# Hybrid encoder step on one core: seven operations of the attention stage change engine or place

## The chip, the cores and the metric

The kernel runs on one core of a Trainium2 chip. The metric is the device time of one execution in microseconds (us), first to last instruction with what lies around it. Engines are named as in the profile: PE is TensorE (PEld its weight loads), DVE is VectorE, ACT is ScalarE, POOL is GpSimd, SP is SyncE, which issues the DMAs here.

## What is computed

One layer is applied to 2048 prompt rows and to 8 sample sequences of 16 rows with 512 cached keys each. This is the reference, cut to the part that the change touches.

```python
def _layer(x, past_k, past_v, ...):
    p = _rms_norm(x, g_pre_mix) @ w_in          # [u | v | q | k | v], 512 columns each
    u_a = gelu(p[..., :512])
    v_a = _layer_norm(gelu(p[..., 512:1024]), ln_v_g, ln_v_b)
    out_a = u_a * (tril(W_s) @ v_a + b)          # gating, chunks of 128 rows, 4 heads
    out_b = _stick_breaking(q, [past_k, k], [past_v, v])   # 8 heads x 64
    mix = concat(_rms_norm(out_a), _rms_norm(out_b)) @ w_out
    x = x + _rms_norm(mix)
    ...                                          # then a convolutional FFN
def _stick_breaking_block(q, k, v):
    z = q @ k.T * 64 ** -0.5
    log_fail = where(reach, log_sigmoid(-z), 0)
    excl = reversed cumulative sum of log_fail, exclusive
    return where(reach, exp(log_sigmoid(z) + excl), 0) @ v
```

## The kernel before

The kernel has four stages, which the profile shows one after the other: the input projection (to about 400 us), attention with the gating branch mixed into it (about 400 to 1126 us), the output projection (to about 1430 us) and the FFN (the rest). Every product of weights and activations that has to be exact in fp32 is made of three fp32r products of a high and a low half (`mm3`, L267 to L269): the high half is a rounding copy, made on ACT, and the low half is the source minus the high half.

**Prompt attention.** `prompt_unit` treats one head, one section of keys and one block of 128 query rows. Its four parts run at a lag to each other in the loop at L863: `pre` six units ahead, `weights_`, `transposes` three units later, `values` after that. `weights_` calls `weigh` (L529): PE makes scores z (L680), ACT makes S = sigmoid(-z) (L543) and s = sigmoid(z) (L544), DVE makes the reversed running product of S in place (L546, a scan) and multiplies s by S shifted by one column (L548). POOL puts the one column at the end of S: a memset to 1 (L536), or a copy of the column `left` (L538) that an earlier section of the same rows left (L688, DVE). `transposes` turns s by PE (L697) and ACT copies it out to T (L698). `values` (L700) multiplies by V for two heads, gg = 0 and 1, each into its own 64 rows of the PSUM tile po (L712 to L715); DVE copies po to ob (L722), which is stored.

**Sample attention.** Eight `sample_unit`s lie among the units of the first head pair. `pre` clears the block-diagonal queries qb on POOL (L565) and fills them from qs by four copies of 64 x 64 (L568), loads cached keys into kr in two parts, rounds them on ACT (L582), takes the low half (L583), and adds the new keys by two small copies (L587). kr has one buffer, so the second part is loaded when the first has been read. `values` copies pos out on ACT (L630), turns it by PE (L632) and writes the two halves into obs (L635).

**Gating.** `gating` is a generator whose steps are spread between the prompt units. `fetch` loads one 128-row block of x into xr (one buffer), rounds it on ACT (L815), takes the low half xl (L816), and 24 products per block follow (L829 to L831); `fetch` of the next block is written ahead of the products of this one. `gate_chain` finishes each block; its one POOL step is rs (L781), on which a DVE step (L783) depends.

The order on each engine is settled at build time by a scheduler that works on a timing model of its own. Within an engine instructions run in that order, and one that waits holds up those behind it. `keep_in_program_order`, used at L582 and L583, keeps an instruction at its written place.

Of the kernel before, what the change touches and what calls it, by code (L numbers as in the profile page):

```python
# [14 lines left out]
F32 = mybir.dt.float32  # L15
F32R = mybir.dt.float32r
AF = mybir.ActivationFunctionType
ALU = mybir.AluOpType
# [8 lines left out]
NB, NS = 8, 16  # L27
# [26 lines left out]
def hybrid_kernel(ctx: ExitStack, tc: tile.TileContext, a: dict):  # L54
    nc = tc.nc
# [4 lines left out]
    def load(out, in_):  # L60

        with ExitStack() as c:
            if loaded:
                c.enter_context(tc.issue_after(loaded[-1]))
            loaded.append(dma(out, in_).ins)
# [24 lines left out]
    ks = lpool.tile([P, 2, 4, NSAMP], F32R, name="ks")  # L90
# [427 lines left out]
    with ExitStack() as c2:  # L518
# [35 lines left out]
        obs = fil.tile([P, 4, NSAMP], F32, name="obs")  # L554

        def sample_unit(b):

            W = PAST + NS
            H = W // 2
            st = {}  # L560

            def pre():
                qb = [fil.tile([P, KD * P], F32R, tag=t, name="qb", bufs=2)[:, :640] for t in ("xh", "xl")]
                for hl in range(2):
                    nc.gpsimd.memset(qb[hl].bitcast(F32), 0.0)  # L565
                    for g in range(2):
                        rows = slice(g * 64, g * 64 + 64)
                        nc.vector.tensor_copy(  # L568
                            qb[hl][rows].rearrange("p (k c) -> p k c", c=160)[:, :, g * NS:(g + 1) * NS],
                            qs[rows, hl, :, b * NS:(b + 1) * NS].bitcast(F32))  # L570
                vnew = fil.tile([P, 512], F32, tag="va", name="vnew", bufs=2)[:NS]
                load(vnew, v_s.parts(b * NS, (b + 1) * NS)[0][0])
                vc = fil.tile([P, 4, 512], F32, tag="ub", name="vc", bufs=2)
                k = []
                for c in range(2):
                    k0, k1 = c * H, min((c + 1) * H, PAST)
                    n = k1 - k0
                    kr = fil.tile([P, 4 * H], F32, tag="xr", name="kr").rearrange("p (k n) -> p k n", k=4)[:, :, :n]
                    load(kr, a["ckT"][b][:, :, k0:k1])
                    hi, lo = (fil.tile([P, 4 * H], F32R, tag=f"fw{2 * c + i}", name=f"ck{i}").rearrange(  # L580
                        "p (k n) -> p k n", k=4) for i in range(2))
                    tc.keep_in_program_order(nc.scalar.copy(hi[:, :, :n], kr))  # L582
                    tc.keep_in_program_order(nc.vector.tensor_tensor(  # L583
                        out=lo[:, :, :n], in0=kr, in1=hi[:, :, :n].bitcast(F32), op=ALU.subtract))
                    if n < H:
                        for hl, kk in enumerate((hi, lo)):
                            nc.vector.tensor_copy(kk[:, :, n:], ks[:, hl, :, b * NS:(b + 1) * NS].bitcast(F32))  # L587
                    k.append((hi, lo))
                load(vc, a["cv"][b])
                st["k"], st["v"] = (qb, k), (vc, vnew)  # L590

            def weights_():
                qb, k = st["k"]

                def fill(z, c0, cn):
                    hi, lo = k[c0 // H]
                    for kt in range(4):
                        q0, q1 = (q[:, kt * P:(kt + 1) * P] for q in qb)
                        mm3(z, q0, q1, hi[:, kt], lo[:, kt], kt == 0, kt == 3 and not c0)
                    if c0:  # L600
                        nc.tensor.matmul(z[:, PAST - c0:], lhsT=identr, rhs=hidesmp, start=False, stop=True)

                st["w"] = weigh(W, H, fill, None)[0]

            def transposes():
                w = st["w"]
                wT = st["wT"] = fil.tile([P, 8 * P], F32, tag="nhl", name="wTs").rearrange("p (j c) -> p j c", c=P)
                pt = pst.tile([P, 4, P], F32, tag="pt", name="pt")
                for j in range(4):
                    nc.tensor.transpose(pt[:, j], w[:, j * P:(j + 1) * P], ident)  # L610
                nc.scalar.copy(wT[:, :4], pt)
                pt = pst.tile([P, 4, P], F32, tag="pt", name="pt")
                nc.tensor.transpose(pt[:NS, 0], w[:, PAST:W], ident)
                nc.scalar.copy(wT[:NS, 4], pt[:NS, 0])

            def values(part):

                if part:
                    return
                vc, vnew = st["v"]  # L620
                wT = st["wT"]
                po = pso.tile([P, 256], F32, tag="po", name="pos")[:, :P]
                for j in range(5):
                    kn = P if j < 4 else NS
                    for kt in range(4):
                        cs = slice(kt * P, (kt + 1) * P)
                        nc.tensor.matmul(po[kt * 32:(kt + 1) * 32], lhsT=wT[:kn, j, kt * 32:(kt + 1) * 32],
                                         rhs=vc[:, j, cs] if j < 4 else vnew[:, cs], start=(j == 0), stop=(j == 4))
                o = fil.tile([P, 512], F32, tag="o", name="os", bufs=2)[:, :P]
                nc.scalar.copy(o, po)  # L630
                pt = pst.tile([P, 4, P], F32, tag="pt", name="pt")
                nc.tensor.transpose(pt[:, 0], o, ident)  # L632
                for g in range(2):
                    rows = slice(g * 64, g * 64 + 64)
                    nc.vector.tensor_copy(obs[rows, :, b * NS:(b + 1) * NS], pt[rows, 0].rearrange(  # L635
                        "p (k c) -> p k c", c=32)[:, :, g * NS:(g + 1) * NS])
                if b == NB - 1:
                    dma(ob_s.parts(0, NSAMP)[0][0].rearrange("f p n -> p f n"), obs)

            return pre, weights_, transposes, values  # L640

        def sections(pr):
# [7 lines left out]
        def prompt_unit(hp, pr, sec, i, g, shared):  # L650
# [3 lines left out]
            n = min(b1, t + 1) - b0  # L654
# [45 lines left out]
            def values(part):  # L700

                if g == 0 or i == 0:
                    return
                cut = [b0 + n * p // NPART for p in range(NPART + 1)]
                if part == 0 and own:
                    shared["po", pr] = pso.tile([P, 2 * P], F32, tag="po", name="po")
                po = shared["po", pr]
                for j in range(cut[part], cut[part + 1]):
                    q = slice(P if j == t else 0, 2 * P)
                    last = j == (b1 - 1 if b0 == 0 else -1)  # L710
                    first_ = own and j == b0
                    for gg in range(2):  # L712
                        T = shared["T", pr, b0 + (j - b0) // 4 * 4, gg]
                        nc.tensor.matmul(po[gg * 64:gg * 64 + 64, q], lhsT=shared["V"][:, j, gg * 64:(gg + 1) * 64],  # L714
                                         rhs=T[:, (j - b0) % 4, q], start=first_, stop=last)  # L715
                if part < NPART - 1 or b0:
                    return
                if ("ob", c) not in shared:
                    shared["ob", c] = two.tile([P, 512], F32, tag="ob", name="ob")
                    shared["n", c] = 0  # L720
                ob = shared["ob", c]
                nc.vector.tensor_copy(ob[:, (pr % 2) * 256:(pr % 2 + 1) * 256], po)  # L722
                shared["n", c] += 1
                if shared["n", c] == 2:
                    dma(ob_s.parts(cs.start, cs.stop)[0][0][hp], ob)

            return pre, weights_, transposes, values, W


# [65 lines left out]
        def gating():  # L795
# [14 lines left out]
            def fetch(i):  # L810
                xr = fil.tile([P, 1056], F32, tag="xr", name="xr")[:, :KD * P].rearrange("p (k n) -> p k n", n=P)
                load(xr, a["xT"][:, :, i * P:(i + 1) * P])
                hi, lo = (fil.tile([P, KD * P], F32R, tag=t, name=t, bufs=2).rearrange("p (k n) -> p k n", n=P)
                          for t in ("xh", "xl"))
                nc.scalar.copy(hi, xr)  # L815
                nc.vector.tensor_tensor(out=lo, in0=xr, in1=hi.bitcast(F32), op=ALU.subtract)  # L816
                return hi, lo

            x = fetch(0)
            n = 0  # L820
            for i in range(NTT):
                if n == 0:
                    n = m = 4 if i < 8 else 3
# [3 lines left out]
                for k in range(KD):  # L827
                    hi, lo, w = x[0][:, k], x[1][:, k], uw[k]
# [501 lines left out]
```

## Time and profile before

| | us |
|---|---|
| median of 3 runs | 2996.64 (2992.61 to 2998.26) |
| the profiled execution: its own time | 2994.9 |
| the profiled execution: span from first to last instruction | 2993.1 |
| PE busy in the span | 2869.0 (96%) |
| DVE busy | 1892.8 (63%) |
| ACT busy | 1347.1 (45%) |
| POOL busy | 343.6 (11%) |

The shares are means over four stages that differ: the FFN is half of the span and keeps PE's weight loads busy nearly all of the time, and the attention stage does not. A PE that is busy by the profile is not a PE at its peak, since matmuls are pipelined and their ends are modelled; the busy share of PEld tells more.

### The profile page before, as it was taken

How to read it: one execution, taken by the hardware profiler on the slowest of the kernel's cores; microseconds unless marked ns; L12 is line 12 of the kernel's file. 1: busy time of each engine (PE TensorE's matmuls, PEld its weight loads, DVE VectorE, ACT ScalarE, POOL GpSimd, SP SyncE). 2: the span in 40 equal slices, each digit the busy share in tenths (PEclk: the TensorE clock that was granted, in tenths of full speed). 3: DMA queues.
4: the chain of work that ended last, by engine and by line, in shares of the span. 5: the costliest groups of instructions: out<-in, count | busy, mean ns of one | idle time of the engine just before them, and what ended most of it. 6: DMA issues, size and time to landing. Idle time of an engine off the chain costs nothing.

```text
span 2993.1 us, 44223 instructions
## 1 busy us (share of the span) xinstructions
PE 2869.0 (96%) x17070; PEld 2627.3 (88%) x17070; DVE 1892.8 (63%) x2840; ACT 1347.1 (45%) x2391; POOL 343.6 (11%) x487
## 2 busy tenths in 40 slices
PE   8999988889999998999999999999999999999997
PEld 7999876657666667999999999899999999999997
DVE  7666668887988894876444555763444476344445
ACT  5444447777767774543332233433232243323222
POOL 0000011011111111552000000310000030000002
PEclk9999989999999999999999999999999999999998
DMA  7767854422434326655222212542212133211223
GB/s 244 241 231 240 255 170 123 117 82 71 126 94 119 86 64 203 225 197 187 67 69 73 64 61 73 152 124 76 70 50 71 61 114 116 78 57 60 75 64 109
DMA packets 242673, 356.06 MB, mean 119 GB/s; under 512 B 26528, under 2 KB 172192, under 8 KB 241440
## 3 DMA queue, kind: packets, MB, share of 16 engines
q1 hardware_dynamic: 242464, 353.24, 38.1%
q8 instruction: 135, 2.21, 0.3%
q14 instruction: 74, 0.61, 0.1%
HBM read 285.66 MB, written 67.51 MB: 118 GB/s over the span
## 4 chain that ended last, share of the span: by engine, by line
PE 79%; DVE 8%; DMA 4%; ACT 4%; issue 3%; POOL 1%; SPq 1%; DVEq 0%; ACTq 0%; POOLq 0%
PE pu L268 12%; PE pu L267 12%; PE pu L269 12%; PE pd L267 5%; PE pd L268 5%; PE pd L269 5%; PE po L714 3%; DVE S L546 3%; PE pt L697 2%; PE psf L267 2%; PE psf L268 2%; PE psf L269 2%; PE z L680 2%; PE pst L385 2%; PE pst L386 2%
## 5 line engine op out<-in xcount | busy, mean ns | idle before, releaser
L185 DVE TENSOR_TENSOR wlo<-wr,whi 128x1024 fp32r<-128x1024 f32 (+2 forms) x325 | 354.3, 1090 | 569.3 <-ACT whi L184 566.9
L267 PE MATMUL pu<-hhi,whi 128*128 128x364 f32 (+1 forms) x2112 | 696.0, 330 | 3.6 <-ACT nhs L1114 3.6
L268 PE MATMUL pu<-hlo,whi 128*128 128x364 f32 (+1 forms) x2112 | 696.8, 330 | 0.0
L269 PE MATMUL pu<-hhi,wlo 128*128 128x364 f32 (+1 forms) x2112 | 696.0, 330 | 0.0
L184 ACT CAST whi<-wr 128x1024 fp32r<-128x1024 f32 (+2 forms) x325 | 296.8, 913 | 709.4 <-PE pu L268 279.0
L267 PEld LDWEIGHTS pu<-hhi,whi 128*128 128x128 f32 x2112 | 399.6, 189 | 4.0 <-ACT nhs L1114 4.0
L268 PEld LDWEIGHTS pu<-hlo,whi 128*128 128x128 f32 x2112 | 399.0, 189 | 0.3 <-POOL hlo L914 0.2
L269 PEld LDWEIGHTS pu<-hhi,wlo 128*128 128x128 f32 x2112 | 398.5, 189 | 0.1
L267 PE MATMUL pd<-ghi,whi 128*128 128x362 f32 (+3 forms) x1016 | 335.1, 330 | 11.4 <-DVE acc L1150 10.9
L269 PE MATMUL pd<-ghi,wlo 128*128 128x362 f32 (+3 forms) x1016 | 334.2, 329 | 0.0
L268 PE MATMUL pd<-glo,whi 128*128 128x362 f32 (+3 forms) x1016 | 334.0, 329 | 0.0
L1102 DVE SCALAR_TENSOR_TENSOR y<-pu,cvec,y 128x726 f32<-128x726 f32 (+2 forms) x352 | 270.0, 778 | 8.7 <-ACT y L1099 4.1
L546 DVE TENSOR_TENSOR_SCAN S<-S 128x896 f32<-128x896 f32 (+8 forms) x136 | 216.2, 1595 | 26.7 <-ACT S L543 26.3
L543 ACT ACTIVATE S<-z 128x512 f32<-128x512 f32 (+4 forms) x336 | 190.2, 570 | 64.5 <-PE z L680 20.4
L697 PEld LDWEIGHTS pt<-ident,s 128*128 128x128 f32 x1088 | 129.2, 147 | 100.3 <-ACT wT L698 38.2
L697 PE MATMUL pt<-ident,s 128*128 128x128 f32 x1088 | 180.8, 291 | 35.7 <-ACT wT L698 16.9
L267 PEld LDWEIGHTS pd<-ghi,whi 128*128 128x128 f32 x1016 | 191.9, 189 | 15.2 <-DVE acc L1150 7.6
L680 PE MATMUL z<-K,Q 128*128 128x512 f32 (+3 forms) x640 | 198.2, 405 | 5.7 <-ACT s L544 3.7
L1150 DVE TENSOR_TENSOR acc<-acc,pd 128x362 f32<-128x362 f32 (+2 forms) x192 | 101.6, 531 | 155.2 <-PE pd L269 154.6
L548 DVE TENSOR_TENSOR s<-s,S 128x640 f32<-128x640 f32 (+7 forms) x200 | 179.4, 901 | 28.3 <-ACT s L544 13.3
L698 ACT COPY wT<-pt 128x512 f32<-128x512 f32 (+3 forms) x320 | 165.3, 553 | 66.2 <-PE pt L697 64.2
L268 PEld LDWEIGHTS pd<-glo,whi 128*128 128x128 f32 x1016 | 191.8, 189 | 0.3
(210 smaller groups left out, 4950.5 us busy)
## 6 DMA issues: line engine op xcount, KB each, us to landing
wr<-wup SPq DMA_DIRECT2D x132, 512.0 KB, 3.4
wk<-win_t SPq DMA_DIRECT2D x96, 256.0 KB, 2.8
wr<-win_f SPq DMA_DIRECT2D x40, 512.0 KB, 5.2
wr<-wout SPq DMA_DIRECT2D x38, 512.0 KB, 4.1
wr<-wdown SPq DMA_DIRECT2D x72, 256.0 KB, 2.7
x<-xT SPq DMA_DIRECT2D x40, 384.0 KB, 5.2
wr<-wdown SPq DMA_DIRECT2D x48, 320.0 KB, 2.9
Q<-q_s SPq DMA_DIRECT2D x112, 128.0 KB, 5.0
```

What stands on the lines that cost most here:

```text
L184: nc.scalar.copy(hi, wr)
L185: nc.vector.tensor_tensor(out=lo, in0=wr, in1=hi.bitcast(F32), op=ALU.subtract)
L267: nc.tensor.matmul(ps, lhsT=whi, rhs=ahi, start=start, stop=False)
L268: nc.tensor.matmul(ps, lhsT=whi, rhs=alo, start=False, stop=False)
L269: nc.tensor.matmul(ps, lhsT=wlo, rhs=ahi, start=False, stop=stop)
L543: nc.scalar.activation(S[:, c0:c0 + cn], z, AF.Sigmoid, scale=-1.0)
L546: nc.vector.tensor_tensor_scan(out=R, data0=R, data1=R, initial=1.0 if carry is None else carry, op0=ALU.mult, op1=ALU.bypass)
L548: nc.vector.tensor_tensor(out=s[:, :W], in0=s[:, :W], in1=S[:, 1:W + 1], op=ALU.mult)
L680: nc.tensor.matmul(z, lhsT=Q[:, j, i * P:(i + 1) * P], rhs=K2[:, b0 * P + c0:b0 * P + c0 + cn], start=(j == 0), stop=(j == 1 and not diago ...
L697: nc.tensor.transpose(pt[:, j], st["w"][:, (j0 - b0 + j) * P:(j0 - b0 + j + 1) * P], ident)
L698: nc.scalar.copy(shared["T", pr, j0, g][:, :jn, i * P:(i + 1) * P], pt[:, :jn])
L1102: nc.vector.scalar_tensor_tensor(out=o, in0=i, scalar=w, in1=o, op0=ALU.mult, op1=ALU.add)
```

## The change

Five DVE operations go to POOL: the copies into qb (L568), the low halves of the cached keys (L583), the copies of the new keys (L587), and the low halves of the gating blocks (L816). (L587 stands for two copies, of high and low half.) Two DVE copies out of PSUM go to ACT: obs (L635) and ob (L722). In `values` the two heads of each pair of products change places. Nothing else differs; the order on every engine is settled anew by the scheduler.

```diff
@@ sample_unit: pre @@
-                        nc.vector.tensor_copy(
+                        nc.gpsimd.tensor_copy(
                             qb[hl][rows].rearrange("p (k c) -> p k c", c=160)[:, :, g * NS:(g + 1) * NS],
                             qs[rows, hl, :, b * NS:(b + 1) * NS].bitcast(F32))
...
-                    tc.keep_in_program_order(nc.vector.tensor_tensor(
+                    tc.keep_in_program_order(nc.gpsimd.tensor_tensor(
                         out=lo[:, :, :n], in0=kr, in1=hi[:, :, :n].bitcast(F32), op=ALU.subtract))
                     if n < H:
                         for hl, kk in enumerate((hi, lo)):
-                            nc.vector.tensor_copy(kk[:, :, n:], ks[:, hl, :, b * NS:(b + 1) * NS].bitcast(F32))
+                            nc.gpsimd.tensor_copy(kk[:, :, n:], ks[:, hl, :, b * NS:(b + 1) * NS].bitcast(F32))
@@ sample_unit: values @@
-                    nc.vector.tensor_copy(obs[rows, :, b * NS:(b + 1) * NS], pt[rows, 0].rearrange(
+                    nc.scalar.copy(obs[rows, :, b * NS:(b + 1) * NS], pt[rows, 0].rearrange(
@@ prompt_unit: values @@
-                    for gg in range(2):
+                    for gg in (1, 0):
...
-                nc.vector.tensor_copy(ob[:, (pr % 2) * 256:(pr % 2 + 1) * 256], po)
+                nc.scalar.copy(ob[:, (pr % 2) * 256:(pr % 2 + 1) * 256], po)
@@ gating: fetch @@
-                nc.vector.tensor_tensor(out=lo, in0=xr, in1=hi.bitcast(F32), op=ALU.subtract)
+                nc.gpsimd.tensor_tensor(out=lo, in0=xr, in1=hi.bitcast(F32), op=ALU.subtract)
```

## Rows read from the trace of the kernel before

**Rows 1.** A window of attention, PE to POOL: engine busy us (instructions), then PEclk, DMA share, GB/s.

```profile
616.00:1126.00 510.00, 478.41 (x2837) 338.88 (x2838) 445.13 (x544) 379.46 (x780) 74.70 (x153) 0.98 0.34 93
```

**Rows 2.** Groups of DVE instructions, 400 to 1126 us: count, busy us, mean ns, idle before.

```profile
L546 DVE TENSOR_TENSOR_SCAN S<-S 128x896 f32<-128x896 f32 (+8 forms) x136 | 216.2, 1595 | 26.7 <-ACT S L543 26.3
L548 DVE TENSOR_TENSOR s<-s,S 128x640 f32<-128x640 f32 (+7 forms) x200 | 179.4, 901 | 28.3 <-ACT s L544 13.3 <-PE pt L697 1.8 <-issue 0.9
L546 DVE TENSOR_TENSOR_SCAN S<-S,left 128x512 f32<-128x512 f32 (+1 forms) x64 | 115.1, 1807 | 4.5 <-ACT S L543 4.3
```

**Rows 3.** The chain of work that ended last, attention: shares; then one piece (start us, us).

```profile
by line: PE po L714 14.0%; DVE S L546 11.0%; issue 9.0%; PE pt L697 9.0%; PE z L680 8.5%; DVE s L548 4.6%; PE pu L831 3.6%; PE pu L829 3.5%; PE pu L830 3.4%; ACT wT L698 3.2%; ACT s L544 3.1%; ACT S L543 3.1%; DMA xr<-xT 2.4%; DMA kr<-ckT 1
...
890.95 1.23 DVE xl L816
```

**Rows 4.** Groups by shape, DVE, 395 to 1430 us: the instructions that move.

```profile
L816 DVE TENSOR_TENSOR xl<-xr,xh 128x1024 fp32r<-128x1024 f32 x17 | 20.7, 1217 | 9.1 <-ACT xh L815 9.1
...
L722 DVE COPY ob<-po 128x256 f32<-128x256 f32 x32 | 13.3, 416 | 6.3 <-PE po L714 6.1
...
L583 DVE TENSOR_TENSOR ck<-kr,ck 128x1056 fp32r<-128x1056 f32 x8 | 10.2, 1274 | 0.7 <-ACT ck L582 0.7
...
L583 DVE TENSOR_TENSOR ck<-kr,ck 128x992 fp32r<-128x992 f32 x8 | 9.5, 1184 | 6.7 <-ACT ck L582 6.6
...
L568 DVE CAST qb<-qs 64x64 fp32r<-64x64 f32 x32 | 6.0, 187 | 0.3
...
L587 DVE CAST ck<-ks 128x64 fp32r<-128x64 f32 x16 | 5.0, 465 | 3.2 <-PE z L268 3.2
...
L635 DVE COPY obs<-pt 64x64 f32<-64x64 f32 x16 | 3.9, 242 | 0.4 <-PE pt L632 0.3
```

**Rows 5.** Groups by shape, POOL, whole span: two-input operations of other stages.

```profile
L256 POOL TENSOR_TENSOR sumy<-sumy,sq 128x470 f32<-128x470 f32 x6 | 7.2, 1200 | 432.9 <-ACT sq L255 432.8
...
L1187 POOL TENSOR_TENSOR xl<-xl,acc 128x470 f32<-128x470 f32 x4 | 4.1, 1017 | 5.2 <-DVE acc L1183 5.2
...
L1187 POOL TENSOR_TENSOR xl<-xl,acc 128x256 f32<-128x256 f32 x4 | 2.6, 640 | 3.0 <-DVE acc L1183 3.0
```

**Rows 6.** Lines L538 and L536 on POOL: duration in ns, min/median/max.

```profile
L538 POOL COPY S<-left x64: 185/1016/2181, 425.3 to 1106.9; 128x1 f32<-128x1 f32 x64
...
L536 POOL MEMSET S<- x136: 93/99/148, 399.7 to 1089.7; 128x1 f32 x136
```

**Rows 7.** Timeline, DVE and POOL side by side: start us, us, what.

```profile
920.94 2.28 DVE L546 TENSOR_TENSOR_SCAN S<-S 128x1024 f32<-128x1024 f32 x1
...
921.18 2.02 POOL L538 COPY S<-left 128x1 f32<-128x1 f32 x1 [4.17 <-DVE left L688]
...
1205.77 1.32 POOL L256 TENSOR_TENSOR sumx<-sumx,sq 128x384 f32<-128x384 f32 x1
...
1206.14 1.36 DVE L256 TENSOR_TENSOR sumb<-sumb,sq 128x384 f32<-128x384 f32 x1
```

**Rows 8.** DVE groups by shape, 395 to 1430 us: one size, two stages.

```profile
L953 DVE TENSOR_TENSOR alo<-ob,ahi 128x384 fp32r<-128x384 f32 x20 | 15.9, 818 | 2.5 <-ACT ahi L952 2.3
...
L462 DVE TENSOR_TENSOR thl<-tf,thl 128x384 fp32r<-128x384 f32 x1 | 0.6, 559 | 0.6 <-ACT thl L461 0.6
```

**Rows 9.** Waits, 400 to 1126 us: total us, times, longest.

```profile
DVE xl L816 <- ACT xh L815: 9.1, 6, 3.1
...
PE pt L697 <- DVE obs L635: 7.3, 6, 2.4
DVE ck L583 <- ACT ck L582: 7.3, 3, 5.0
...
PE pos L627 <- DVE ob L722: 2.1, 2, 1.1
PE po L714 <- ACT wT L698: 1.9, 5, 0.8
```

**Rows 10.** ACT groups by shape: a 256-column copy out of PSUM.

```profile
L698 ACT COPY wT<-pt 128x256 f32<-128x256 f32 x32 | 13.4, 421 | 4.0 <-PE pt L697 4.0
```

## The prediction

> **What bounds the kernel now.** Only attention (400 to 1126 us) is touched, so I read the windows of that stage first [rows 1]. From 616 us on PE is busy 478 of 510 us, but its weight loads only 339, so PE does not stream at its peak there: it waits in small pieces. DVE is busy 445 of 510 us (87%); ACT 379 of 510 (74%). DVE is the fullest engine behind PE. What it does is the scan and the multiply behind it, 216.2 + 115.1 us for the scans (two forms of the line) and 179.4 us for the multiplies [rows 2]; both read two operands from SBUF. The chain of waits then says how much of the stage hangs on DVE: the scan is 11.0% and the multiply 4.6% of it, PE's five largest lines 38.6%, ACT's three 9.4% [rows 3]. With DVE's smaller lines I take a quarter: **one us of DVE time is worth about 0.25 us of span**, and the same for a stall of DVE. That is my choice, and the weakest number here; in single stretches it is nearer to a half.
>
> **DVE work removed.** By their rows [rows 4]: xl 17 x 1.217 = 20.7 us, ck low halves 10.2 + 9.5 = 19.7, qb copies 6.0, new-key copies 5.0, ob 13.3, obs 3.9: 68.6 us, of which 51.4 go to POOL and 17.2 to ACT.
>
> **What POOL takes for it.** The trace has no POOL operation of 1024 columns. In the quiet tail POOL takes 1.017 us for 470 columns and 0.640 for 256, that is 1.76 ns a column, and 1.017 + 554 x 0.00176 = 1.99 us for 1024. Another POOL line took 1.200 us at 470; scaled by the same 1.99 / 1.017 it gives 2.4 [rows 5]. I take 2.2 us, between them. (The Trainium skill, GPSIMD Engine Reference, section 3.1, measured 4497 ns for such an add at 2048 columns; half of that is an estimate of 2.25 us. The range does not rest on it.) So 33 operations of 2.2 us, 73 us, take the place of 40.4 us on DVE.
>
> **They do not run beside DVE.** The copy of one column on POOL takes 0.185 us at best, but 1.016 us in the median and up to 2.181; the memset beside it, which reads nothing, never more than 0.148 [rows 6]. The timeline shows why: a copy starts at 921.18 and ends at 923.20, and the DVE scan that started at 920.94 ends at 923.22 [rows 7]. POOL's read waited for the scan's end. It holds the other way too: DVE's add of 384 columns at 1206.14 took 1.36 us, while a POOL add ran from 1205.77 to 1207.09; undisturbed this size takes 0.56 us [rows 7, 8]. They take turns, and nearly all of DVE's work in attention is of the kind that takes turns.
>
> By that, a POOL operation that reads SBUF waits for the DVE instruction it meets (median 1.016 - 0.185 = 0.8 us), and then DVE's next one waits for it. How much DVE loses per operation is the disputed number. Lower bound: nothing, POOL falls into DVE's gaps. Upper: 2.4 us, all of it. DVE has something to do 0.85 of the time, so I take 2.2 x 0.85 = 1.9 us less some one-operand work that may run beside it: 1.8. For the 48 small copies I take 0.2 us each (the undisturbed 0.185 for one column, and few columns more): 10 us. DVE then loses 33 x 1.8 + 10 = 69 us and is spared 68.6. **The load of DVE stays where it is: 0 us**, with bounds of -68.6 x 0.25 = -17 and (80 + 10 - 68.6) x 0.25 = +5.
>
> (The Trainium skill, SBUF — State Buffer, "Who interferes with whom", says that a DVE instruction with two SBUF inputs and a GpSimd instruction that reads SBUF shut each other out for a whole instruction. The rows above agree. Were it not so, DVE would gain the full 68.6 us, 17 us of span; that is the lower bound just given, and it makes the third case below.)
>
> **Latency of the low halves.** xl lies on the chain where the first xl product follows it at once, as after the piece at 890.95, 1.23 us [rows 3]. On POOL it is 2.2 - 1.2 = 1.0 us longer and waits 0.8 us for DVE's instruction, against the place in DVE's queue that it no longer waits for. I count 3 such places for xl and ck together and 1.5 us each: **+4 us**; bounds 0 (all covered by the lead of one block) and 8 pieces, which is what I see of both lines on the chain, x 1.8 = +14. kr and xr have one buffer each, so the load behind a low half, and SP's later loads of queries behind that, start as much later; the block of lead hides it for xr, and for kr it is inside this bound.
>
> **Stalls that leave DVE.** DVE is in order, and waited 9.1 us for ACT's half of xl and 7.3 for that of ck [rows 9], 3.2 us ahead of the new-key copies. These 19.6 us go to POOL. At 0.25 that is **-5 us**; bounds -10 and 0. Behind the waiting instruction on POOL now stand the memsets and copies of S's last column, and rs. The column is wanted by the multiply, a scan later, and S has three buffers, so some 4 to 5 us cover it; rs is wanted at once by DVE, 17 times. With 33 operations of 3 us in 726 us a rs meets one every seventh time: under 1 us in all. If the cover of S fails for every one of the 33, by half an operation (1.6 us), DVE stands 53 us, 13 us of span. **+1 us**, bounds 0 and +13.
>
> **Evacuations on ACT.** PE waited 7.3 us for obs to free a transpose buffer and 2.1 us for ob to free po [rows 9]. ACT's instructions are shorter than a scan, so its queue comes round sooner: I take back half, **-4 us**; bounds -9 and +3. ACT takes 0.421 us for 256 columns [rows 10] against 0.416 on DVE, so 32 x 0.42 + 16 x 0.25 = 17.4 us more on an engine that is 74% busy; at ACT's share of the chain (0.1, doubled because a wait for po now holds up the sigmoids behind it) **+3 us**, bounds 0 and +6.
>
> **Order of the heads.** The second head's T is the last to be copied out. Where the products wait for it, the first head's no longer fill the wait, at most 0.2 us in each; PE stood 1.9 us in 5 such waits [rows 9], 5 x 0.2 = 1. **+1 us**, bounds -2 and +3.
>
> **Sum:** 0 + 4 - 5 + 1 - 4 + 3 + 1 = 0 us, and I add 2 us since the scheduler's order is settled by a timing model that need not know of the turns, so that an instruction behind a POOL result stands where the result is not ready yet. The profiled execution took 2994.9 us (span 2993.1 and 1.8 around it), 1.7 under the median of 2996.64; the forecast for the median is **2999 us**.
>
> **The rivals.**
>
> *The turns cost more than the moved work (slower).* For: in stretches with a full DVE queue, strict alternation, as at 1205.77. Then each POOL operation costs DVE its whole 2.2 us: 33 x 2.2 + 10 - 68.6 = +14 us; where DVE's scans are the chain half of that shows, +7. The waits at xl and ck come to the upper half (+9), and some S columns come late (+6); minus 9 for the stalls and PE's waits, plus 4 for ACT and the heads: +17, **3014 us**. It decides from about 1.8 us of lost DVE time per POOL operation on. Against: DVE idles 13%.
>
> *DVE is really relieved (faster).* For: in the output projection, where POOL works on long operations too, DVE's 384-column subtractions rose from 0.559 to 0.818 us only [rows 8], so about a quarter of POOL's time came out of DVE, not 0.8. Then DVE loses 73 x 0.27 + 3 = 23 us and is spared 68.6: -46 x 0.25 = -11; stalls -5, PE's waits -5, latency, ACT and heads +5: -16, **2980 us**. Against: there only some of DVE's work reads two operands, in attention nearly all.
>
> **How the numbers follow.** The first case (2990 to 3008) has a chance of 0.43, the slower rival 0.25, the faster one 0.32: the relief is certain, its price is inferred. A measurement of this kernel can tell about 0.2%, 6 us, from no change: 2990.6 to 3002.6 is "same". Of the first case 0.29 lies there, 0.13 above and 0.01 below. So faster 0.33, same 0.29, slower 0.38. The range, 8 in 10, runs from 2974 to 3024, cutting the ends of both rivals; the likeliest case's own is 2990 to 3008.
>
> **What would show it.** The moved operations on POOL: about 2.2 us where DVE is idle, 3 in the mean. Scans and multiplies that overlap them: longer by up to 2 us, and the means of those two DVE lines (1595, 1807 and 901 ns) up by some 0.15 to 0.2 us; if they stay where they are, the third case holds. DVE's waits for ACT's halves: gone. PE's waits for obs and ob: less than half. Waits for POOL's S column: under 5 us; over 20 would be the slower rival. PE's waits for xl: up by a few us. Input projection and FFN: unchanged, to 2 us. I am wrong altogether if the scheduler's new order shifts the stage by more than these waits explain.

## The result, and the profile after

The changed kernel takes 3008.01 us in the median of 7 runs (3002.97 to 3017.28), the kernel before 2994.24 in 7 runs beside it: a ratio of **1.0054, 95% interval 1.0043 to 1.0066**, slower by 16 us (the medians lie 14 us apart). The forecast was 2999 with a range of 2974 to 3024; the time lies in the range, on the slower side.

The profiled execution of after has a span of 3001.1 us, 8.0 more than before. The input projection is unchanged. Attention, from 400 us to the start of the last copy of po to ob, ends at 1138.5 instead of 1126.5 us, and what follows takes 1862.6 instead of 1866.6 us.

After, a window of attention as in [rows 1]: busy us of PE, PEld, DVE, ACT, POOL with their instructions, PEclk, DMA share, GB/s.

```profile
616.00:1126.00 510.00, 451.95 (x2801) 330.54 (x2800) 438.62 (x500) 381.84 (x803) 112.44 (x170) 0.96 0.34 92
```

PE and DVE are both less busy than before, POOL is busier by 38 us, and the stage is longer all the same. So no engine has become full: waits have grown. PE also has less to do (its value products take 152.8 us in the whole stage and not 185.9, as shown below), and it runs more slowly: the clock granted to it (PEclk) is 0.96 of full speed in this window and was 0.98.

After, groups of DVE and then of POOL instructions in attention (count | busy us, mean ns | idle before), to set beside [rows 2, 4].

```profile
L546 DVE TENSOR_TENSOR_SCAN S<-S 128x896 f32<-128x896 f32 (+8 forms) x136 | 228.5, 1683 | 54.5 <-ACT S L543 54.2
L548 DVE TENSOR_TENSOR s<-s,S 128x640 f32<-128x640 f32 (+7 forms) x200 | 208.2, 1044 | 43.5 <-ACT s L544 15.2 <-PE z L680 8.7 <-POOL qb L565 3.1
L546 DVE TENSOR_TENSOR_SCAN S<-S,left 128x512 f32<-128x512 f32 (+1 forms) x64 | 120.0, 1884 | 2.4 <-ACT S L543 2.4
...
L816 POOL TENSOR_TENSOR xl<-xr,xh 128x1024 fp32r<-128x1024 f32 x17 | 46.9, 2759 | 24.3 <-ACT xh L815 24.0
L583 POOL TENSOR_TENSOR ck<-kr,ck 128x1056 fp32r<-128x1056 f32 x8 | 24.8, 3102 | 1.7 <-ACT ck L582 1.6
L583 POOL TENSOR_TENSOR ck<-kr,ck 128x992 fp32r<-128x992 f32 x8 | 24.7, 3090 | 5.5 <-ACT ck L582 5.3
L568 POOL CAST qb<-qs 64x64 fp32r<-64x64 f32 x32 | 14.8, 464 | 1.3
```

The same scans and multiplies take 12.3 + 28.8 + 4.9 = 46.0 us longer, while 68.6 us of other work have left DVE. And DVE's scans now wait 54.2 us for ACT's S where they waited 26.3: DVE has time, but its input comes late.

After, one low half on POOL beside DVE: start us, us, what.

```profile
895.88 2.35 DVE L546 TENSOR_TENSOR_SCAN S<-S,left 128x1024 f32<-128x1024 f32 x1
898.35 3.12 DVE L548 TENSOR_TENSOR s<-s,S 128x1024 f32<-128x1024 f32 x1
...
896.22 4.17 POOL L816 TENSOR_TENSOR xl<-xr,xh 128x1024 fp32r<-128x1024 f32 x1
```

POOL is issued at 896.22, waits for the scan to end at 898.23, and works until 900.39; the multiply, ready at 898.35, ends at 901.47 and not at 899.58, where the 1.23 us that it takes undisturbed would have put it. Both stand, one after the other.

After, waits in attention (total us, times, longest), to set beside [rows 9].

```profile
DVE S L546 <- ACT S L543: 56.5, 36, 12.0
...
POOL xl L816 <- ACT xh L815: 24.0, 9, 4.3
...
PE pn L787 <- DVE o L783: 16.9, 7, 5.0
...
PE po L714 <- ACT wT L698: 12.7, 17, 3.3
...
ACT ob L722 <- PE po L714: 10.1, 10, 3.6
...
PE pt L697 <- ACT obs L635: 9.3, 5, 4.5
```

DVE no longer waits for the rounding copies of xl and ck; POOL does. PE waits more for T (12.7 against 1.9 us) and for obs (9.3 against 7.3).

### The profile page after: what moved, and what is told of

It is laid out like the page before. It is cut to its first block, busy times and chain, and to the rows that moved or that the text cites. A ratio compares the mean times of both kernels' runs of the same rounds, so it can differ in the third digit from the quotient of the medians.

```text
span 3001.1 us, 44303 instructions
## 1 busy us (share of the span) xinstructions
PE 2841.1 (95%) x17070; PEld 2619.4 (87%) x17070; DVE 1881.9 (63%) x2711; ACT 1355.6 (45%) x2439; POOL 455.2 (15%) x568
## 4 chain that ended last, share of the span: by engine, by line
PE 76%; DVE 8%; DMA 6%; ACT 4%; issue 4%; POOL 1%; SPq 1%; DVEq 0%; ACTq 0%; POOLq 0%
PE pu L268 12%; PE pu L269 12%; PE pu L267 12%; PE pd L267 5%; PE pd L269 5%; PE pd L268 5%; PE po L714 3%; DVE S L546 3%; PE z L680 2%; PE pt L697 2%; PE pst L385 2%; PE pst L386 2%; PE psm L269 2%; PE psm L267 2%; PE psm L268 2%
## 5 line engine op out<-in xcount | busy, mean ns | idle before, releaser
L546 DVE TENSOR_TENSOR_SCAN S<-S 128x896 f32<-128x896 f32 (+8 forms) x136 | 228.5, 1683 | 54.5 <-ACT S L543 54.2
L548 DVE TENSOR_TENSOR s<-s,S 128x640 f32<-128x640 f32 (+7 forms) x200 | 208.2, 1044 | 43.5 <-ACT s L544 15.2
L544 ACT ACTIVATE s<-z 128x512 f32<-128x512 f32 (+4 forms) x336 | 193.8, 582 | 0.0
```

Source lines behind the costliest of these rows:

```text
L544: nc.scalar.activation(s[:, c0:c0 + cn], z, AF.Sigmoid)
L546: nc.vector.tensor_tensor_scan(out=R, data0=R, data1=R, initial=1.0 if carry is None else carry, op0=ALU.mult, op1=ALU.bypass)
L548: nc.vector.tensor_tensor(out=s[:, :W], in0=s[:, :W], in1=S[:, 1:W + 1], op=ALU.mult)
```

## The experiments

Twelve kernels. Each takes some parts of the change, or replaces one. Called *xl*: gating low halves on POOL; *sample*: cached-key low halves, qb and new-key copies on POOL; *copies*: obs and ob on ACT; *heads*: the order of the value products. "us" is the ratio times 2992, the median of before beside these runs. The two last columns are from the one profiled execution each: the length of attention, from 400 us to the last copy of po, against 726.5 of before, and of what follows it. One execution can lie some us off its kernel's median: that of before lies 3 us above its median here, that of heads 5 above, those of after and of copies, heads 5 and 7 below. Differences of a few us in these columns say nothing.

| kernel | ratio (95% interval) | us | attention | rest |
|---|---|---|---|---|
| before | 1 | 0 | 726.5 | 1866.6 |
| xl | 1.0000 (0.9990 to 1.0009) | 0 | +4.2 | 1857.1 |
| sample | 1.0032 (1.0022 to 1.0043) | +10 | +12.7 | 1857.2 |
| copies | 0.9960 (0.9947 to 0.9972) | -12 | -5.8 | 1857.7 |
| heads | 0.9930 (0.9917 to 0.9944) | -21 | -13.4 | 1860.7 |
| xl, copies, heads | 1.0007 (0.9999 to 1.0016) | +2 | +1.4 | 1861.9 |
| xl, sample, heads | 1.0033 (1.0020 to 1.0045) | +10 | +9.5 | 1860.8 |
| xl, sample, copies | 1.0035 (1.0022 to 1.0048) | +10 | +17.8 | 1859.8 |
| copies, heads | 0.9970 (0.9960 to 0.9979) | -9 | -15.0 | 1861.8 |
| xl written, not read | 0.9979 (0.9969 to 0.9988) | -6 | -6.1 | 1861.1 |
| heads, first of four | 0.9952 (0.9939 to 0.9964) | -14 | -10.4 | 1860.6 |
| heads, obs | 0.9932 (0.9918 to 0.9945) | -20 | -18.2 | 1862.4 |
| small copies | 0.9981 (0.9972 to 0.9990) | -6 | -2.7 | 1861.1 |
| after (all parts) | 1.0054 (1.0043 to 1.0066) | +16 | +12.0 | 1862.6 |

### Each part alone

The theory was that of the prediction, the turns of POOL and DVE; the rival, that the copies on ACT make the loss.

```diff
@@ xl @@
-                nc.vector.tensor_tensor(out=lo, in0=xr, in1=hi.bitcast(F32), op=ALU.subtract)
+                nc.gpsimd.tensor_tensor(out=lo, in0=xr, in1=hi.bitcast(F32), op=ALU.subtract)
```

> Only the 17 low halves of the gating blocks go to GpSimd. Turns theory (GpSimd reads and VectorE two-operand work exclude each other): the 17 operations take about 2.4 us each (mean over 2.6 with waits), the means of the VectorE scans and multiplies rise by some 17 x 1.8 = 30 us in sum while 20.7 us are removed, and the time moves by 0 to +5 us. ACT theory (the loss of the whole change comes from the two copies moved to ScalarE): the same relief of 20.7 us is worth something here, -5 to 0 us. If GpSimd ran beside VectorE, scans and multiplies would keep their means and the time would fall by about 5 us.

xl alone, DVE groups in attention, then xl on POOL:

```profile
L546 DVE TENSOR_TENSOR_SCAN S<-S 128x896 f32<-128x896 f32 (+8 forms) x136 | 219.9, 1620 | 29.1 <-ACT S L543 28.9
L548 DVE TENSOR_TENSOR s<-s,S 128x640 f32<-128x640 f32 (+7 forms) x200 | 197.0, 989 | 24.9 <-ACT s L544 10.7 <-PE pt L697 1.8 <-issue 0.9
L546 DVE TENSOR_TENSOR_SCAN S<-S,left 128x512 f32<-128x512 f32 (+1 forms) x64 | 116.7, 1830 | 8.9 <-ACT S L543 8.7
...
L816 POOL TENSOR_TENSOR xl<-xr,xh 128x1024 fp32r<-128x1024 f32 x17 | 48.2, 2832 | 29.7 <-ACT xh L815 25.5 <-PE z L680 4.1
```

Scans and multiplies rise by 3.7 + 17.6 + 1.6 = 22.9 us, 1.35 us for each of the 17 operations, and 20.7 us are removed. The time does not move.

```diff
@@ sample @@
-                        nc.vector.tensor_copy(
+                        nc.gpsimd.tensor_copy(
                             qb[hl][rows]...
-                    tc.keep_in_program_order(nc.vector.tensor_tensor(
+                    tc.keep_in_program_order(nc.gpsimd.tensor_tensor(
                         out=lo[:, :, :n], ...
-                            nc.vector.tensor_copy(kk[:, :, n:], ...
+                            nc.gpsimd.tensor_copy(kk[:, :, n:], ...
```

> Only the sample units' three operations (low halves of cached keys, copies into qb, copies of new keys) go to GpSimd. Turns theory: scans and multiplies before 616 us grow by some 16 x 1.8 + 10 = 39 us while 30.7 us are removed; with the longer wait for the key halves the time rises by 3 to 8 us. ACT theory: about 0 us or below.

Slower by 10 us, a little more than the turns theory had, and not by its arithmetic: scans and multiplies rose by 24.8 us, less than the 30.7 us removed. What was lost is looked for below.

```diff
@@ copies @@
-                    nc.vector.tensor_copy(obs[rows, ...
+                    nc.scalar.copy(obs[rows, ...
-                nc.vector.tensor_copy(ob[:, ...
+                nc.scalar.copy(ob[:, ...
```

> Only the two copies out of PSUM (obs, ob) go to ScalarE. Turns theory: no GpSimd read is added, so VectorE is relieved of 17.2 us and the time falls by 0 to 5 us. ACT theory: ScalarE stands some 10 us for the products, the sigmoids and copies behind it come late, and this part alone gives most of the change's loss, +6 to +13 us.

Faster by 12 us, so the rival falls as far as this part alone goes; the turns theory, with 0 to 5 us, falls short as well. PE's transposes wait 2.1 us for obs here, against 7.3 before [rows 9].

```diff
@@ heads @@
-                    for gg in range(2):
+                    for gg in (1, 0):
```

> Only the order of the two heads in the value products changes. The forecast's step: +1 us (-2 to +3), nothing that can be measured. Rival: a product of the first head no longer runs alone ahead of its partner, so pairs stay together and PE gains 2 to 6 us.

Faster by 21 us, far more than either expectation, and the largest effect of all. The reason stands in PE's order.

Before, then heads alone, PE around the same products: start us, us, line, count.

```profile
728.52 0.65 PE L714 MATMUL po<-wT,V 128*64 128x256 f32 x2
729.09 0.73 PE L680 MATMUL z<-K,Q 128*128 128x512 f32 x2
...
732.52 1.94 PE L714 MATMUL po<-wT,V 128*64 128x256 f32 x14
734.40 0.33 PE L697 MATMUL pt<-ident,s 128*128 128x128 f32 x1
```
```profile
726.82 1.95 PE L714 MATMUL po<-wT,V 128*64 128x256 f32 x16
728.70 0.98 PE L697 MATMUL pt<-ident,s 128*128 128x128 f32 x7
```

One product is two of the trace's matmuls. Eight products in one run, the two heads by turns, take 1.88 us from their start to the next line's, 0.235 each. Before, a product stands alone (0.57 us until the next line starts), and the run of the other seven takes 1.88 us all the same. The two heads write to different halves of PE's columns, and a product whose partner follows at once overlaps with it (in the trace the two start 0.007 us apart, at 732.525 and 732.532, and take 0.43 us each); one that went ahead, and the one it left behind, do not. In the order of PE's instructions 68 products stand alone before and one after the change of order, in 169 and 109 runs. The group rows show the sum: before, heads alone, after, in this order.

```profile
L714 PE MATMUL po<-wT,V 128*64 128x256 f32 (+1 forms) x1152 | 185.9, 383 | 2.6 <-ACT wT L698 1.9
```
```profile
L714 PE MATMUL po<-wT,V 128*64 128x256 f32 (+1 forms) x1152 | 144.2, 380 | 6.5 <-ACT wT L698 6.3
```
```profile
L714 PE MATMUL po<-wT,V 128*64 128x256 f32 (+1 forms) x1152 | 152.8, 399 | 12.7 <-ACT wT L698 12.7
```

Of the 42 us of PE's time that heads alone saves, 21 show in the time of the kernel.

### One group left out

The parts alone sum to 0 + 10 - 12 - 21 = -23 us, the whole is +16. So four combinations.

> The whole change without the sample units' three GpSimd operations (kept: gating low halves on GpSimd, both copies on ScalarE, heads changed). If the parts simply add, as measured alone: 0.0 - 12 - 21 = -33 us against before. If the sample units' GpSimd work is what spoils the whole, it comes near that; if not, it stays near or above before.

> The whole change without the two copies on ScalarE. If the parts add: 0 + 9 - 21 = -12 us. If copies on ScalarE become harmful once GpSimd makes VectorE late (ScalarE stands in order for products that wait for a late T), this kernel is -12 us while the whole change is +14.

> The whole change without the changed order of the heads. If the parts add: 0 + 9 - 12 = -3 us. If the whole products' run behind the last T is what meets the late VectorE (the products can no longer start with the first head), this kernel is near -3 us while the whole is +14.

> Copies on ScalarE and heads changed, nothing on GpSimd. If the parts add: -12 - 21 = -33 us, 2960 us, faster than both kernels. If these two spoil each other (ScalarE holds both the copies of T and those of the products), it is slower than the heads alone (2971 us).

No single group spoils the whole: without sample +2, without copies +10, without heads +10, all above the sum of their parts. Copies and heads without any POOL move give -9, slower than heads alone, so these two spoil each other in part. Two things come out of the table's last columns, and a third out of the clock.

First, the rest: what follows attention takes 1866.6 us in the profile of before and 1857 to 1863 in that of every other kernel. Each part alone has this gain once, the sum of four parts counts it four times. It makes 30 of the 44 us that the profiled spans leave between whole (+8.0) and sum (-36.0); the other 14 lie in attention. Some 9 of the 44 are only the 3 us by which the execution of before was slow, counted three times too often. What shortens the rest is open. In before PE waits 7.2 us for the gating result to come back from memory when the output projection starts; in xl and in copies this wait is gone, but in sample it is 6.4 us, and its rest is as short as theirs.

Second, within attention xl and sample together cost 17 us as the sum of both alone, 23 with heads, 24 with copies, 27 with both. The gains of copies and heads shrink beside them. So the POOL moves are a loss in every combination: with copies and heads in place they turn -9 us into +16.

Third, the clock granted to PE, which no expectation took into account. It has two levels, 2.4 and 1.2 GHz. At the first a run of eight products takes 1.88 us (above). In after one takes 3.61 us at the second, behind a wait of 3.28 us for T. PE's timeline, then a window around it as in [rows 1]:

```profile
663.66 3.68 PE L714 MATMUL po<-wT,V 128*64 128x256 f32 x16 [3.28 <-ACT wT L698]
667.27 0.48 PE L697 MATMUL pt<-ident,s 128*128 128x128 f32 x1
...
662.20:668.60 6.40, 4.94 (x22) 2.72 (x24) 5.45 (x6) 3.01 (x7) 0.20 (x2) 0.50 0.16 44
```

The mean granted clock of an execution is 0.985 in the median of before and 0.982 or more in that of ten of the other kernels. In the three that have both the heads and low halves on POOL it is lower: 0.980 (xl, copies, heads), 0.975 (xl, sample, heads) and 0.977 (after). Between 400 and 1150 us PE is busy for 80.5 us at 1.2 GHz in the profile of after and for 54.8 in that of before. The same products take about half the time at 2.4 GHz, so these 26 us more are an estimated loss of up to 13 us, nearly as much as the 14 us in attention that the parts do not explain. This is not shown to be the cause: a PE that waits is late by the wait as well, and no run parted the two.

### Reading or only working

```diff
-                nc.vector.tensor_tensor(out=lo, in0=xr, in1=hi.bitcast(F32), op=ALU.subtract)
+                for _ in range(2):
+                    nc.gpsimd.memset(lo.bitcast(F32), 0.0)
```

> Left out: the low halves of the gating blocks are not computed; GpSimd writes zeros over them twice (two operations of about 1.0 us, which read nothing) in place of its subtraction of 2.4 us. Turns theory: the means of VectorE's scans and multiplies go back to those of before (1595, 1807 and 901 ns), against 1620, 1830 and 989 with the subtraction on GpSimd. If any GpSimd work of that length slowed VectorE, the means would stay near the latter. The time also loses the wait for the rounding copy, so it is read for the means, not for the sum; I expect -10 to 0 us.

xl written, not read: DVE groups in attention, then the writes on POOL.

```profile
L546 DVE TENSOR_TENSOR_SCAN S<-S 128x896 f32<-128x896 f32 (+8 forms) x136 | 216.4, 1595 | 36.6 <-ACT S L543 36.3
L548 DVE TENSOR_TENSOR s<-s,S 128x640 f32<-128x640 f32 (+7 forms) x200 | 179.5, 901 | 23.7 <-ACT s L544 9.2 <-PE pt L697 2.2 <-issue 0.6
L546 DVE TENSOR_TENSOR_SCAN S<-S,left 128x512 f32<-128x512 f32 (+1 forms) x64 | 115.4, 1809 | 9.4 <-ACT S L543 9.3
...
L817 POOL MEMSET xl<- 128x1024 f32 x34 | 32.4, 953 | 31.2 <-PE pu L832 23.3 <-PE z L269 4.9 <-PE z L601 2.5
```

34 POOL operations of 0.95 us leave DVE's means where they were before, to 2 ns, and none of them takes longer than 0.96 us; 17 subtractions raised the multiply's mean by 88 ns, and took 2.36 to 4.25 us themselves. It is POOL's reading that takes turns with DVE. This is what the Trainium skill says in SBUF — State Buffer, "Who interferes with whom", for a DVE instruction with two SBUF inputs, and here the trace shows it for the scan too. Between the two kernels lie 6 us of time, for which the turns (22.9 us of DVE) and the wait for the rounding copy stand together.

### What the sample units lose

```diff
@@ small copies @@
-                        nc.vector.tensor_copy(
+                        nc.gpsimd.tensor_copy(
                             qb[hl][rows]...
-                            nc.vector.tensor_copy(kk[:, :, n:], ...
+                            nc.gpsimd.tensor_copy(kk[:, :, n:], ...
```

> Only the 48 small copies of the sample units (qb, new keys) go to GpSimd, the low halves of the cached keys stay on VectorE. If the sample units' loss of 9 us is the low halves' (turns and 2 us of latency each), this kernel is within 3 us of before. If it is the small copies, +5 us or more.

The 48 small copies alone gain 6 us (the expectation had been within 3), and the scans and multiplies do not rise (510.9 us in sum against 510.7). So the 16 low halves of the cached keys cost some 15 us, the difference of the two kernels. They hold up the load behind them, because kr has one buffer. Waits of SP's queue between 396 and 626 us, the two issues of one unit's keys (start us, us), all issues of keys (durations in ns; first and last start), and PE's wait for obs: small copies, then sample.

```profile
SPq L65 <- DVE ck L583: 50.9, 9, 11.9
...
437.08 7.71 SPq L65 DMA_DIRECT2D kr<-ckT  x2
...
L65 SPq DMA_DIRECT2D kr<-ckT x16: 566/570/620, 403.4 to 571.2; - x16
...
PE pt L697 <- DVE obs L635: 8.3, 6, 3.6
```
```profile
SPq L65 <- POOL ck L583: 61.2, 10, 12.4
...
438.40 12.42 SPq L65 DMA_DIRECT2D kr<-ckT  x2
...
446.84 3.38 POOL L583 TENSOR_TENSOR ck<-kr,ck 128x1056 fp32r<-128x1056 f32 x1
...
L65 SPq DMA_DIRECT2D kr<-ckT x16: 546/570/619, 404.6 to 585.7; - x16
...
PE pt L697 <- DVE obs L635: 16.9, 7, 5.7
```

The second part's load is issued when the low half of the first is done, and the loads of values and queries stand behind it on SP. In the kernel after this wait is 73.4 us. The first load of keys is issued 1.2 us later in sample than in small copies, the last one 14.5 us later: what the two kernels differ by has come in by the end of the sample units. PE's own waits for the low half are small (1.9 us), while its wait for obs, which DVE copies here, doubles. That the wait for kr sets the pace, and the loads are not late with all the rest, is argued and not shown: no kernel with two buffers of kr was run.

### The heads and the copies

```diff
-                    for gg in range(2):
+                    for gg in ((1, 0) if (j - b0) % 4 == 0 or j == cut[part] else (0, 1)):
```

> Of the change only the heads' order, and of that only the first product of each group of four key blocks (one T tile holds four); the others keep the first head in front. If the gain of the heads (-21 us, half as many and longer runs of products) comes from the wait for the T that is copied last standing in front of the run, this kernel has it too: -15 to -21 us and some 125 runs of products instead of 185. If it comes from the order of the two column halves on TensorE, a third of it at most: -7 us or less.

-14 us (-10 to -18): most of the gain, if a little less than expected, with 2 lone products in 109 runs. So what matters is that the run waits for the T copied last. Its products take 149.5 us of PE, 5.3 more than heads alone. The order inside a run is not the reason, for a run of eight takes 1.88 us here too (727.85 to 729.73); but 11.4 us of these products were done at 1.2 GHz, and 3.7 us in heads alone, which makes some 4 of the 5.3 us by estimate. The rest of the 7 us that lack is open.

> Heads changed and only the sample units' copy obs on ScalarE; ob stays on VectorE. If ob on ScalarE (which stands in order for the last product) is what makes copies and heads together slower than heads alone, this kernel keeps the sample units' gain and loses nothing after 616 us: 2960 to 2968 us. If obs is the cause: 2975 us or more.

2972.32 us against 2971.05 of heads alone, one time as far as these runs tell, and between the two expectations; with ob on ACT as well it is 2982.38. So ob is what copies and heads together suffer from. Waits in attention: copies and heads, then heads and obs.

```profile
DVE S L546 <- ACT S L543: 42.2, 30, 4.5
PE z L680 <- ACT s L544: 13.7, 24, 2.2
PE po L714 <- ACT wT L698: 11.9, 18, 3.2
ACT ob L722 <- PE po L714: 7.6, 9, 2.3
```
```profile
DVE S L546 <- ACT S L543: 26.0, 22, 4.5
PE z L680 <- ACT s L544: 10.1, 19, 2.3
...
PE po L714 <- ACT wT L698: 6.8, 17, 1.4
```

With ob, ACT stands 7.6 us for the products' end, its sigmoids come later for DVE's scans by 16 us of waiting, and T for PE by 5. Whether these waits are the loss is not shown: copies alone has as much of the first two (ACT waits 13.5 us for the products, DVE 42.9 for S) and is faster than before. **The best version is heads alone, 2971 us**, or with obs on ACT: faster by 0.7% than before and by 1.2% than after.

## Why the prediction held, and which of its steps did not

The time came out in the range and on the forecast's side, but 9 us above the forecast, at the upper edge of the likeliest case and near the time of the slower rival (3014). The forecast was 2 us more than before; it became 16 by the ratio. The steps:

- **Turns.** Right as a mechanism, shown by the writes that read nothing. POOL's operation was put at 2.2 us and 3 with waits; it takes 2.3 at least and 2.76 to 3.1 in the mean. The loss of DVE was mis-sized: 1.8 us per low half forecast, 46.0 / 33 = 1.4 measured, and 10 us for the small copies, measured 0. The means rose by 0.08 to 0.14 us, where 0.15 to 0.2 was the sign. DVE was relieved of some 23 us, not 0.
- **Latency of the low halves.** The term that failed: +4 us forecast, with +14 as its bound and the one buffer of kr "inside this bound". The cached keys alone cost 15 us, of which their turns explain little: scans and multiplies rose by 24.8 us and 19.7 us of low halves left DVE. The 6 us that xl costs against writes cannot be put to latency alone, since the turns are in them. I had counted pieces of the chain where the low half itself stood; the next load waits on SP for the buffer, and over the sample units the loads of keys fall 13 us behind. That the buffer is the reason is likely and not shown.
- **Stalls that leave DVE.** They left DVE (16.4 us before; POOL has 30.8 us of waits for rounding copies now), but the scans' wait for ACT's S rose by 26 us: what DVE got free in the whole, it waited. That does not refute the price of 0.25 for one us of DVE. In xl written, not read, 20.7 us of work and 9.1 us of waits left DVE and nothing took turns with it; the price makes that 7 us, and the time fell by 6.
- **S's column and rs.** The cover held. DVE's multiply waited for POOL once, 3.1 us, which the profile puts down to the clearing of qb, and the forecast's sign was under 5; for rs DVE waited 6.7 us against 6.0.
- **Evacuations on ACT.** Forecast -4 + 3 = -1 us; alone they give -12, of which the table puts 6 in attention. Beside the new order of the heads ob on ACT is a loss of 11 us. In the whole PE's wait for obs did not halve but rose to 9.3 us.
- **Order of the heads.** Forecast +1 with a bound of -2; alone -21. The 0.2 us that each wait was to cost stands on no row; what a product without its partner costs does, 0.57 us where 0.235 would do. The step called it a merit of the old order that the first head's products fill the wait. The row that spoke against it was in the timeline (runs of two, then of fourteen), and I read the durations of products without their neighbours.
- **The added 2 us** for an order settled on a timing model. What it stood for was larger: parts and whole differ by 39 us, part of it in what follows the stage, and part of it perhaps in the granted clock.
- **The slower rival** came near in time but not in its mechanism: it wanted the whole 2.2 us of each POOL operation from DVE, and from 1.8 on.

That +4, +1 and -1 were all wrong by 11 to 22 us and of both signs is why the sum came out near: the time was right by luck. What is open: why copies and heads, which gain 33 us apart, gain so little beside the POOL moves. PE's waits for ACT grow there and its granted clock falls, but no run took either away.

## What to carry to other kernels

An operation moved to POOL does not run beside a DVE that is busy with two-operand SBUF work; it takes its turn, and its longer time stands in every load that waits for its buffer. Before a low half is moved, look at how many buffers its source has and what is queued behind the next load. Where two products can share the array, have both ready before the first is issued: a product that went ahead to fill a wait cost more than the wait here. When parts do not add up, compare the granted clock of the kernels as well as their waits.

## What the runs showed that I had not expected

Products for the two column halves of PE overlap when they follow each other: 0.235 us each in a run of eight, 0.57 us for one that stands alone. The same run takes 3.61 us and not 1.88 when it meets the lower clock. A POOL copy of 64 columns, which waits for DVE's turn (0.46 us in the mean, 0.23 at least), costs DVE nothing that its means show, while a subtraction of 1024 columns costs 1.4 us.
